# Two float32 half chunks per turn in place of one float32 chunk, in the narrow expert positions of an encoder trunk

## The chip, the cores and the metric

The kernel runs on one core of one Trainium2 chip. The metric is the device time of one execution in microseconds, the median of several runs; lower is better. Engines are named as the profile names them: PE is TensorE (matmuls), PEld its weight loads, DVE is VectorE, ACT is ScalarE, POOL is GpSimd, SP is SyncE, which here issues the weight loads from memory.

## The reference, cut to what matters

A two-layer encoder trunk on 256 tokens of width 1024. The part that the change touches is the last block, a mixture of eight SwiGLU experts of which each token takes two:

```python
def swiglu(xn, w_gu, w_down):
    g, u = jnp.split(xn @ w_gu, 2, axis=-1)
    return (jax.nn.silu(g) * u) @ w_down

def moe_swiglu(xn, router, w_gu, w_down):
    logits = (xn @ router).astype(jnp.float32)
    top_v, top_i = lax.top_k(logits, TOP_K)
    w = jax.nn.softmax(top_v, axis=-1)
    ...
    for e in range(N_EXPERTS):
        out = out + comb[..., e:e + 1] * swiglu(xn, w_gu[e], w_down[e])
    return out
```

`w_gu[e]` is 1024 x 7168 (gate and up side by side), `w_down[e]` is 3584 x 1024, all float32.

## The kernel before

**Precision.** A weight chunk is 128 x 2048 float32 (1 MB): four blocks of 128 x 512. `split` (line 152) cuts it into two halves of two blocks and, for each half, makes a rounded part `hi` on ACT (line 168, a cast to float32r) and a rest `lo = raw - hi` on DVE (line 169). Matmuls then run in float32r, one pass per block and part. `hi` and `lo` halves live in rings of four buffers each (lines 87, 88, `NPART = 4`), which is two chunks' worth; a buffer comes free when PE has read it. Raw chunks live in 11 buffers of one pool and 6 of another (line 55), 17 in all, loaded in order by SP (lines 143 and 939).

**Positions and turns.** The eight experts stand in eight positions, which `expert` (line 1127) takes one after the other. Positions 2, 4 and 6 are narrow (`NARROW`): their expert gets at most 64 tokens, and the activations' `hi` and `lo` stand side by side in one 128-column tile, so that one stationary tile carries both. The others are wide: 128 token slots, `hi` and `lo` in two tiles, so each block takes three passes (`moving`, line 207) where a narrow one takes two (`narrow`, line 1118: all `hi` blocks of a chunk, then all `lo` blocks).

A position has seven turns (loop at line 1208), one for each 512 columns of the hidden width. A turn takes six chunks in the order of their loads: two of the gate product (below: a, b), two of the up product (c, d), two of the down product of the turn before (e, f). In a narrow turn before the change, chunk d is not split: `gate_up` (line 1132) takes it with `whole_chunk` (line 1110) and runs four float32 matmuls on the raw data (line 1139; the trace shows two matmul records per block). The other five chunks are split: ten casts on ACT and ten subtractions on DVE per turn.

**What happens to a gate product in a narrow turn** (`gate`, line 1152): two copies on ACT bring the two 64-row halves of the result across (lines 1156, 1157), DVE adds them to the product (1158), ACT takes the silu (1159), and DVE multiplies with the up product (1163). `to_rows` (line 1166) turns that result by eight small matmuls (1172), which `side_by_side` (line 1049) casts on ACT (1053) and subtracts on DVE (1054); this is the stationary operand of the next `down` (line 1180).

**What sets the order.** The engines' instruction streams are not written out by hand. The framework's scheduler orders each engine's stream when the program is built, by program order as priority and by what its own timing model says is ready; each engine then runs its stream strictly in that order. `tc.issue_after(ins)` keeps what a block traces on the engine of `ins` behind `ins` in that stream, without a wait. `done[0]` is the last cast on ACT that `split` traced.

Of the kernel before, what the change touches and what calls it, by code (L numbers as in the profile page):

```python
# [25 lines left out]
F32 = mybir.dt.float32  # L26
F32R = mybir.dt.float32r
I32 = mybir.dt.int32
AF = mybir.ActivationFunctionType
# [3 lines left out]
P = 128  # L33
# [6 lines left out]
NE = 8  # L40
# [4 lines left out]
CH = 2048  # L45
# [4 lines left out]
HALF = CAP // 2  # L50
# [31 lines left out]
def _build(ctx, tc, io, cap):  # L82
# [7 lines left out]
    work = ctx.enter_context(tc.tile_pool(name="work", bufs=2))  # L90
    w2b, w1b = 4, 5
# [6 lines left out]
    V, S, G, PE = nc.vector, nc.scalar, nc.gpsimd, nc.tensor  # L98

    def f32(ap):  # L100
        return ap.bitcast(F32)
# [4 lines left out]
    def acc_tile(name="acc"):  # L106
        return psA.tile([P, 512], F32, tag="acc", name=name)
# [20 lines left out]
    def col(name, i=0):  # L128
        o = _OFF[name] + i
        return vec[:, o:o + 1]  # L130
# [18 lines left out]

    done = []  # L150

    def split(raw, n=CH, pieces=2, apart=()):

        cut = (n // 2 + P - 1) // P * P
        parts = []
        for a, b in ((0, cut), (cut, n)):
            if len(parts) in apart:  # L160
                both = rawp.tile([P, CH], F32R, tag="raw", name="apart")
                hi, lo = both[:, :CH // 2], both[:, CH // 2:]
            else:
                hi = hip.tile([P, CH // 2], F32R, tag="hi", name="hi")
                lo = lop.tile([P, CH // 2], F32R, tag="lo", name="lo")
            step = (b - a) * 2 // pieces
            for i in range(0, b - a, step):
                done[:] = (S.copy(hi[:, i:i + step], raw[:, a + i:a + i + step]),  # L168
                           V.tensor_sub(lo[:, i:i + step], raw[:, a + i:a + i + step],  # L169
                                        f32(hi[:, i:i + step])))  # L170
            parts.append((hi, lo))

        def at(a, b):
            hi, lo = parts[a >= cut]
            o = cut if a >= cut else 0
            return hi[:, a - o:b - o], lo[:, a - o:b - o]
        return at
# [44 lines left out]
    def halves(ps):  # L222
        return ps.rearrange("p (m t) -> p m t", m=2)
# [60 lines left out]
    def whole_of(t):  # L284
        return lambda k: t[:, k * T:(k + 1) * T]
# [269 lines left out]
    for g, w in enumerate(POOL_WINDOWS):  # L555
        left, right = w // 2, w - 1 - w // 2
        G.memset(invc[:, g, :], 1.0 / w)
        for t in list(range(left)) + list(range(T - right, T)):
            n = min(t + right, T - 1) + 1 - max(t - left, 0)
# [142 lines left out]
    ps = None  # L702
    for m in range(KD):
        if m % 2 == 0:
            ps = halves(acc_tile())
# [4 lines left out]
        for hf in range(2):  # L710
            w = split(load(io["ffn_down"][m, hf], half * P), half * P)
# [3 lines left out]
            for kk in range(half):  # L715
                k = hf * half + kk
                h, sl = hid[k // 8], slice((k % 8) * T, (k % 8 + 1) * T)
# [22 lines left out]
    for k in range(KD):  # L740
        last = V.scalar_tensor_tensor(a3[:, k * T:(k + 1) * T], hT[:, k, :], col("od_norm_mix", k), rb,
                               op0=ALU.mult, op1=ALU.mult)
    pw1 = [load(io["pw1"][c]) for c in range(2)]
    with tc.issue_after(last.ins):
        k1.append(split(load(io["wk"][1, 2])))
        ws = [Early(load(io["wv"][1, 2]), act_pair("wv")), early[2]]
# [44 lines left out]
    for c in range(KD):  # L791
        ps = product_whole(pw1[c] if c < 2 else load(io["pw1"][c]), whole_of(a3))
# [5 lines left out]
    last = conv31(KD - 1)  # L798
# [5 lines left out]
    ws = early[:2] + ws  # L804
# [18 lines left out]
    with tc.issue_after(last.ins):  # L823
        w = split(load(io["pw2"][0]))
# [21 lines left out]
    for k in range(KD):  # L846
# [5 lines left out]
        last = V.tensor_sub(p2[1][:, sl], x1, f32(p2[0][:, sl]))  # L852
# [5 lines left out]
    for c in range(1, 4):  # L858
        with tc.issue_after(last.ins):
            w = split(load(io["pw2"][c]))  # L860
# [75 lines left out]
    ahead = deque()  # L936
# [19 lines left out]
    for c in (1, 2):  # L956
        with tc.issue_after(turned[0].ins), tc.issue_after(turned[1].ins):
            w = split(wos[c])
# [148 lines left out]
    xg = big_tile("xg", F32R)  # L1107
    ht = big_tile("ht", F32R)

    def whole_chunk():  # L1110
        if not ahead:
            fetch()
        return ahead.popleft()

    def chunk(pieces=2):
        return split(whole_chunk(), pieces=pieces)

    def narrow(ps, xs, ws, first, last):

        n = len(xs)  # L1120
        for part in range(2):
            for i, (x, w) in enumerate(zip(xs, ws)):
                ins = PE.matmul(ps, x, w[part], start=first and i == part == 0,  # L1123
                                stop=last and part == 1 and i == n - 1)
        return ins

    def expert(e, g, following):
        nonlocal fn
        py = out_tiles()
        two = e in NARROW  # L1130

        def gate_up(j, gu):
            pz = acc_tile("gu")
            for kh in range(2):
                xs = [xg[:, k * P:(k + 1) * P] for k in range(kh * 4, kh * 4 + 4)]
                if two and gu == kh == 1:
                    w = whole_chunk()
                    for kk in range(4):
                        PE.matmul(pz, f32(xs[kk]), w[:, kk * 512:(kk + 1) * 512],  # L1139
                                  start=False, stop=kk == 3)  # L1140
                    continue
                w = chunk()
                ws = [w(kk * 512, (kk + 1) * 512) for kk in range(4)]
                if two:
                    narrow(pz, xs, ws, kh == 0, kh == 1)
                    continue
                moving(pz, [(xg[:, k * P:(k + 1) * P], xg[:, D + k * P:D + (k + 1) * P])
                            for k in range(kh * 4, kh * 4 + 4)],
                       ws, kh == 0, kh == 1)
            return pz  # L1150

        def gate(pg, pu):
            sg = work.tile([P, 512], F32, tag="w2", name="esg", bufs=w2b)
            if two:

                S.copy(sg[:HALF], pg[HALF:])
                S.copy(sg[HALF:], pg[:HALF])
                V.tensor_add(sg, sg, pg)
                S.activation(sg, sg, AF.Silu, scale=g.cw[:, 1:2])
            else:  # L1160
                S.activation(sg, pg, AF.Silu, scale=g.cw[:, 1:2])
            h = work.tile([P, 512], F32, tag="w2", name="eh", bufs=w2b)
            V.scalar_tensor_tensor(h, pu, g.cw[:, 1:2], sg, op0=ALU.mult, op1=ALU.mult)
            return h
# [12 lines left out]
            S.copy(ht[:, o:o + 512], pt)  # L1177
            V.tensor_sub(ht[:, o + 512:o + D], pt, f32(ht[:, o:o + 512]))

        def down(j, n):  # L1180
            w = chunk(4 if e == NE - 1 and j == 6 else 2)
            o = (j % 2) * D
            if two:
                return narrow(py[n], [ht[:, o + f * P:o + (f + 1) * P] for f in range(4)],
                              [w(f * 512, (f + 1) * 512) for f in range(4)], j == 0, j == 6)
            return moving(py[n],
                   [(ht[:, o + f * P:o + (f + 1) * P], ht[:, o + 512 + f * P:o + 512 + (f + 1) * P])
                    for f in range(4)],
                   [w(f * 512, (f + 1) * 512) for f in range(4)], j == 0, j == 6)
# [17 lines left out]
        h = None  # L1207
        for j in range(7):
            pg = gate_up(j, 0)
            if j:  # L1210
                to_rows(j - 1, h)
            pu = gate_up(j, 1)
            h = gate(pg, pu)
            if j:
                down(j - 1, 0)
                if j == 6:
                    to_rows(6, h)
                down(j - 1, 1)
            if following is not None and j in (3, 5):
                following.step(j)  # L1220
# [7 lines left out]
        last = down(6, 1)  # L1228
# [9 lines left out]
    g = Gather(0)  # L1238
# [88 lines left out]
    for e in range(NE):  # L1327
        following = Gather(e + 1) if e + 1 < NE else None
        expert(e, g, following)
        g = following  # L1330
# [174 lines left out]
```

## Time and profile before

| what | value |
|---|---|
| median of 3 runs | 1547.85 us (1547.59 to 1548.0) |
| the profiled execution, device time | 1547.42 us |
| its span in the trace | 1545.7 us |
| mean granted TensorE clock | 0.996 |
| DVE busy over the span | 1298.9 us (84%) |
| ACT busy over the span | 1052.1 us (68%) |
| POOL busy over the span | 148.1 us (10%) |

The profiled execution lasted 1.7 us longer than its span (launch and end lie outside) and 0.4 us less than the median. Busy shares are averages over stages with different limits: the expert block lies from about 591 us to 1532 us of the span, and its narrow and wide positions have to be read apart. A matmul's end in the trace is modelled, so the pace of PE is read from start to start.

### The profile page before, as it was taken

Reading aid. Unit: us, or ns where it says so; the run is one execution under the profiler, and the core shown is the slowest. Engines: PE = TensorE matmul, PEld = TensorE weight load, DVE = VectorE, ACT = ScalarE, POOL = GpSimd, SP = SyncE. Lnnn points to the kernel's source line nnn. Section 1 sums busy time; section 2 is a strip of 40 time slices with the busy share of each in tenths; the row PEclk is TensorE's granted clock in tenths of the full one; section 3 lists DMA queues with packets and bytes.
Section 4 is the critical chain, followed back from the end, with each engine's and each line's share of the span. In section 5 each row is a group of like instructions: output and inputs, shape, how many; then the busy total and the mean of one; then the engine's idle time right before and its main releaser. Section 6 shows DMA issues by size and latency. Waiting matters only on the chain.

```text
span 1545.7 us, 23643 instructions
## 1 busy us (share of the span) xinstructions
PE 1511.9 (98%) x8558; PEld 1294.3 (84%) x8558; DVE 1298.9 (84%) x1735; ACT 1052.1 (68%) x1381; POOL 148.1 (10%) x230
## 2 busy tenths in 40 slices
PE   8999999999999999999999999999999999999996
PEld 8899999999998998888888768888667888667885
DVE  7876677776898868999999989889889888889897
ACT  6555554455585647777777877777777777777775
POOL 4710100001394210000000000000000000000000
PEclk9999999999999999999999999999999999999998
DMA  9654454336536566998999999998999999999950
GB/s 370 269 191 164 142 186 166 120 113 236 188 134 244 174 264 221 371 377 334 373 366 342 397 422 412 381 375 331 403 402 376 367 361 343 408 392 382 364 191 30
DMA packets 65213, 451.42 MB, mean 292 GB/s; under 512 B 7360, under 2 KB 7488, under 8 KB 12480
## 3 DMA queue, kind: packets, MB, share of 16 engines
q1 hardware_dynamic: 65088, 449.83, 76.6%
q8 instruction: 69, 1.13, 0.3%
q14 instruction: 56, 0.46, 0.1%
HBM read 448.75 MB, written 1.05 MB: 291 GB/s over the span
## 4 chain that ended last, share of the span: by engine, by line
PE 82%; DVE 9%; POOL 3%; issue 3%; ACT 2%; DMA 1%; SPq 0%; DVEq 0%; POOLq 0%; ACTq 0%
PE gu L211 8%; PE gu L212 8%; PE gu L216 8%; PE acc L205 7%; PE acc L203 7%; PE acc L204 7%; DVE lo L169 6%; PE gu L1139 5%; PE gu L1123 4%; PE py L211 4%; PE py L216 4%; PE py L212 4%; PE py L1123 3%; POOL part L779 2%; PE gx L1042 1%
## 5 line engine op out<-in xcount | busy, mean ns | idle before, releaser
L169 DVE TENSOR_TENSOR lo<-raw,hi 128x1024 fp32r<-128x1024 f32 (+3 forms) x573 | 671.6, 1208 | 113.9 <-ACT hi L168 103.6
L168 ACT CAST hi<-raw 128x1024 fp32r<-128x1024 f32 (+3 forms) x573 | 565.4, 1030 | 212.9 <-PE acc L204 89.4
L169 DVE TENSOR_TENSOR lo<-spare,hi 128x1024 fp32r<-128x1024 f32 (+1 forms) x226 | 260.9, 1198 | 24.4 <-ACT hi L168 20.4
L168 ACT CAST hi<-spare 128x1024 fp32r<-128x1024 f32 (+1 forms) x226 | 221.5, 1035 | 23.6 <-PE gu L212 11.7
L211 PE MATMUL gu<-hi,xg 128*128 128x512 f32 x560 | 218.8, 391 | 0.0
L212 PE MATMUL gu<-hi,xg 128*128 128x512 f32 x560 | 218.3, 390 | 0.0
L216 PE MATMUL gu<-lo,xg 128*128 128x512 f32 x560 | 154.2, 391 | 0.6 <-DVE lo L169 0.6
L216 PEld LDWEIGHTS gu<-lo,xg 128*128 128x128 f32 x560 | 104.7, 188 | 23.9 <-DVE lo L169 1.9
L211 PEld LDWEIGHTS gu<-hi,xg 128*128 128x128 f32 x560 | 105.1, 188 | 22.2 <-ACT hi L168 0.2
L212 PEld LDWEIGHTS gu<-hi,xg 128*128 128x128 f32 x560 | 105.1, 188 | 21.8
L211 PE MATMUL py<-hi,ht 128*128 128x512 f32 x280 | 111.1, 398 | 0.0
L212 PE MATMUL py<-hi,ht 128*128 128x512 f32 x280 | 109.3, 390 | 0.0
L205 PE MATMUL acc<-a2h,lo 128*128 128x256 f32 x336 | 95.2, 283 | 0.0
L204 PE MATMUL acc<-a2l,hi 128*128 128x256 f32 x336 | 95.2, 283 | 0.0
L203 PE MATMUL acc<-a2h,hi 128*128 128x256 f32 x336 | 95.1, 283 | 0.0
L1401 POOL TENSOR_TENSOR fo<-accum,fn 128x512 f32<-128x512 f32 x2 | 2.5, 1272 | 948.9 <-DVE accum L1205 948.9
L1123 PE MATMUL gu<-lo,xg 128*128 128x512 f32 x252 | 80.4, 411 | 7.9 <-DVE lo L169 7.6
L216 PE MATMUL py<-lo,ht 128*128 128x512 f32 x280 | 84.0, 395 | 0.0
L1123 PE MATMUL gu<-hi,xg 128*128 128x512 f32 x252 | 71.3, 397 | 0.0
L1123 PEld LDWEIGHTS gu<-lo,xg 128*128 128x128 f32 x252 | 43.4, 188 | 31.5 <-DVE lo L169 25.2
L203 PEld LDWEIGHTS acc<-a2h,hi 128*128 128x128 f32 x336 | 64.5, 192 | 0.0
L205 PEld LDWEIGHTS acc<-a2h,lo 128*128 128x128 f32 x336 | 64.5, 192 | 0.0
(424 smaller groups left out, 3171.9 us busy)
## 6 DMA issues: line engine op xcount, KB each, us to landing
raw<-in_moe_gu SPq DMA_DIRECT2D x139, 1024.0 KB, 7.1
spare<-in_moe_gu SPq DMA_DIRECT2D x85, 1024.0 KB, 7.2
raw<-in_moe_down SPq DMA_DIRECT2D x78, 1024.0 KB, 7.4
spare<-in_moe_down SPq DMA_DIRECT2D x32, 1024.0 KB, 7.0
raw<-in_ffn_gu SPq DMA_DIRECT2D x22, 1024.0 KB, 4.8
raw<-in_pw SPq DMA_DIRECT2D x12, 1024.0 KB, 4.8
raw<-in_ffn_down SPq DMA_DIRECT2D x16, 704.0 KB, 4.1
raw<-in_wk SPq DMA_DIRECT2D x8, 1024.0 KB, 7.3
```

The lines of the kernel that those rows point to most:

```text
L168: done[:] = (S.copy(hi[:, i:i + step], raw[:, a + i:a + i + step]), V.tensor_sub(lo[:, i:i + step], raw[:, a + i:a + i + step], f32(hi[:, ...
L169: V.tensor_sub(lo[:, i:i + step], raw[:, a + i:a + i + step], f32(hi[:, i:i + step])))
L203: PE.matmul(ps, a[0], b[0], start=first, stop=False)
L204: PE.matmul(ps, a[0], b[1], start=False, stop=False)
L205: PE.matmul(ps, a[1], b[0], start=False, stop=last)
L211: PE.matmul(ps, a[0], b[0], start=first and i == 0, stop=False)
L212: PE.matmul(ps, a[1], b[0], start=False, stop=False)
L216: ins = PE.matmul(ps, a[0], b[1], start=False, stop=last and i == n - 1)
L779: G.tensor_add(part, part, prod)
L1042: PE.matmul(px[:, kk * P:(kk + 1) * P], xt[:, t * D + d0:t * D + d0 + P], oh[:, t, :], start=t == 0, stop=t == 1)
L1123: ins = PE.matmul(ps, x, w[part], start=first and i == part == 0, stop=last and part == 1 and i == n - 1)
L1139: PE.matmul(pz, f32(xs[kk]), w[:, kk * 512:(kk + 1) * 512], start=False, stop=kk == 3)
```

## The change

In a narrow turn, all six chunks now go through `split`, which learns to leave one of its halves whole (`whole=(1,)`: no cast, no subtraction; the raw half is handed out). The second half of chunk c (the first chunk of the up product) and the second half of chunk f (the second chunk of the down product) are left whole, and chunk d is split. `narrow` takes the blocks with a `hi` and a `lo` first and then the raw blocks, as float32. The two copies and the addition of the gate product move out of `gate` into `fold`, which is traced right after chunk c is split, with the copies queued on ACT behind the cast of c's first half. Silu is queued on ACT behind the casts of chunk e, which is therefore split ahead of `gate`. Wide positions keep their code.

```diff
--- before.py
+++ after.py
@@ -149,7 +149,8 @@
 
     done = []
 
-    def split(raw, n=CH, pieces=2, apart=()):
+    def split(raw, n=CH, pieces=2, apart=(), whole=()):
+
 
 
 
@@ -157,6 +158,9 @@
         cut = (n // 2 + P - 1) // P * P
         parts = []
         for a, b in ((0, cut), (cut, n)):
+            if len(parts) in whole:
+                parts.append(None)
+                continue
             if len(parts) in apart:
                 both = rawp.tile([P, CH], F32R, tag="raw", name="apart")
                 hi, lo = both[:, :CH // 2], both[:, CH // 2:]
@@ -171,6 +175,8 @@
             parts.append((hi, lo))
 
         def at(a, b):
+            if parts[a >= cut] is None:
+                return raw[:, a:b]
             hi, lo = parts[a >= cut]
             o = cut if a >= cut else 0
             return hi[:, a - o:b - o], lo[:, a - o:b - o]
@@ -1107,21 +1113,17 @@
     xg = big_tile("xg", F32R)
     ht = big_tile("ht", F32R)
 
-    def whole_chunk():
+    def chunk(pieces=2, whole=()):
         if not ahead:
             fetch()
-        return ahead.popleft()
-
-    def chunk(pieces=2):
-        return split(whole_chunk(), pieces=pieces)
+        return split(ahead.popleft(), pieces=pieces, whole=whole)
 
     def narrow(ps, xs, ws, first, last):
 
-        n = len(xs)
-        for part in range(2):
-            for i, (x, w) in enumerate(zip(xs, ws)):
-                ins = PE.matmul(ps, x, w[part], start=first and i == part == 0,
-                                stop=last and part == 1 and i == n - 1)
+        todo = [(x, w[part]) for part in range(2) for x, w in zip(xs, ws) if isinstance(w, tuple)]
+        todo += [(f32(x), w) for x, w in zip(xs, ws) if not isinstance(w, tuple)]
+        for i, (x, w) in enumerate(todo):
+            ins = PE.matmul(ps, x, w, start=first and i == 0, stop=last and i == len(todo) - 1)
         return ins
 
     def expert(e, g, following):
@@ -1129,36 +1131,35 @@
         py = out_tiles()
         two = e in NARROW
 
-        def gate_up(j, gu):
+        def gate_up(j, gu, pg=None):
             pz = acc_tile("gu")
             for kh in range(2):
                 xs = [xg[:, k * P:(k + 1) * P] for k in range(kh * 4, kh * 4 + 4)]
-                if two and gu == kh == 1:
-                    w = whole_chunk()
-                    for kk in range(4):
-                        PE.matmul(pz, f32(xs[kk]), w[:, kk * 512:(kk + 1) * 512],
-                                  start=False, stop=kk == 3)
-                    continue
-                w = chunk()
+                w = chunk(whole=(1,) if two and gu and kh == 0 else ())
                 ws = [w(kk * 512, (kk + 1) * 512) for kk in range(4)]
+                if two and gu and kh == 0:
+
+                    with tc.issue_after(done[0].ins):
+                        pg = fold(pg)
                 if two:
                     narrow(pz, xs, ws, kh == 0, kh == 1)
                     continue
                 moving(pz, [(xg[:, k * P:(k + 1) * P], xg[:, D + k * P:D + (k + 1) * P])
                             for k in range(kh * 4, kh * 4 + 4)],
                        ws, kh == 0, kh == 1)
-            return pz
+            return (pg, pz) if gu else pz
+
+        def fold(pg):
+
+            sg = work.tile([P, 512], F32, tag="w2", name="esg", bufs=w2b)
+            S.copy(sg[:HALF], pg[HALF:])
+            S.copy(sg[HALF:], pg[:HALF])
+            V.tensor_add(sg, sg, pg)
+            return sg
 
         def gate(pg, pu):
-            sg = work.tile([P, 512], F32, tag="w2", name="esg", bufs=w2b)
-            if two:
-
-                S.copy(sg[:HALF], pg[HALF:])
-                S.copy(sg[HALF:], pg[:HALF])
-                V.tensor_add(sg, sg, pg)
-                S.activation(sg, sg, AF.Silu, scale=g.cw[:, 1:2])
-            else:
-                S.activation(sg, pg, AF.Silu, scale=g.cw[:, 1:2])
+            sg = pg if two else work.tile([P, 512], F32, tag="w2", name="esg", bufs=w2b)
+            S.activation(sg, pg, AF.Silu, scale=g.cw[:, 1:2])
             h = work.tile([P, 512], F32, tag="w2", name="eh", bufs=w2b)
             V.scalar_tensor_tensor(h, pu, g.cw[:, 1:2], sg, op0=ALU.mult, op1=ALU.mult)
             return h
@@ -1177,8 +1178,9 @@
             S.copy(ht[:, o:o + 512], pt)
             V.tensor_sub(ht[:, o + 512:o + D], pt, f32(ht[:, o:o + 512]))
 
-        def down(j, n):
-            w = chunk(4 if e == NE - 1 and j == 6 else 2)
+        def down(j, n, w=None):
+            if w is None:
+                w = chunk(4 if e == NE - 1 and j == 6 else 2, (1,) if two and n else ())
             o = (j % 2) * D
             if two:
                 return narrow(py[n], [ht[:, o + f * P:o + (f + 1) * P] for f in range(4)],
@@ -1209,10 +1211,12 @@
             pg = gate_up(j, 0)
             if j:
                 to_rows(j - 1, h)
-            pu = gate_up(j, 1)
-            h = gate(pg, pu)
+            pg, pu = gate_up(j, 1, pg)
+            w = chunk() if j and two else None
+            with tc.issue_after(done[0].ins) if two else nullcontext():
+                h = gate(pg, pu)
             if j:
-                down(j - 1, 0)
+                down(j - 1, 0, w)
                 if j == 6:
                     to_rows(6, h)
                 down(j - 1, 1)
```

## Rows read from the trace of the kernel before

**Rows 1.** The page, part 1: busy time of PE and PEld (share) over the whole span.

```profile
PE 1511.9 (98%) x8558; PEld 1294.3 (84%) x8558; DVE 1298.9 (84%) x1735; ACT 1052.1 (68%) x1381; POOL 148.1 (10%) x230
```

**Rows 2.** Windows, positions 2, 3, 4, 6: us, PE, PEld, DVE, ACT, POOL busy, clock, DMA, GB/s.

```profile
838.00:940.00 102.00, 101.15 (x437) 74.38 (x437) 94.16 (x100) 82.89 (x101) 0.00 (x0) 1.00 1.00 400
940.00:1067.00 127.00, 126.81 (x591) 105.12 (x590) 115.73 (x115) 97.01 (x109) 0.00 (x0) 1.00 0.98 378
1067.00:1175.00 108.00, 103.89 (x429) 71.16 (x428) 92.24 (x98) 79.82 (x98) 0.00 (x0) 1.00 0.97 388
...
1302.00:1410.00 108.00, 103.93 (x429) 71.17 (x428) 92.48 (x96) 79.95 (x99) 0.00 (x0) 1.00 0.98 391
```

**Rows 3.** Windows view, single turns: one of position 4, two of position 2.

```profile
1109.34:1124.90 15.56, 14.71 (x58) 9.53 (x56) 13.11 (x14) 11.73 (x14) 0.00 (x0) 1.00 0.99 395
...
873.40:886.40 13.00, 13.00 (x56) 9.55 (x55) 12.88 (x13) 11.70 (x14) 0.00 (x0) 1.00 0.96 377
886.40:899.40 13.00, 13.00 (x56) 9.54 (x55) 12.72 (x13) 11.23 (x14) 0.00 (x0) 1.00 1.01 425
```

**Rows 4.** Timeline of ACT, position 4: start, us, instruction, count, [idle before, releaser].

```profile
1110.89 0.59 ACT L1156 COPY esg<-gu 64x512 f32<-64x512 f32 x1 [1.58 <-PE gu L1123]
...
1112.96 0.72 ACT L1159 ACTIVATE esg<-esg,cw 128x512 f32<-128x512 f32 x1 [0.90 <-DVE esg L1158]
1113.59 1.97 ACT L168 CAST hi<-spare 128x1024 fp32r<-128x1024 f32 x2
...
1118.83 0.37 ACT L1053 CAST ht<-ht 128x256 fp32r<-128x256 f32 x1 [1.36 <-PE ht L1172]
1119.09 5.79 ACT L168 CAST hi<-raw 128x1024 fp32r<-128x1024 f32 x6
1126.44 0.58 ACT L1156 COPY esg<-gu 64x512 f32<-64x512 f32 x1 [1.55 <-PE gu L1123]
1127.04 0.58 ACT L1157 COPY esg<-gu 64x512 f32<-64x512 f32 x1
```

**Rows 5.** Timeline of DVE, the same turn.

```profile
1112.25 0.68 DVE L1158 TENSOR_TENSOR esg<-esg,gu 128x512 f32<-128x512 f32 x1
1114.65 1.23 DVE L169 TENSOR_TENSOR lo<-spare,hi 128x1024 fp32r<-128x1024 f32 x1 [1.72 <-ACT hi L168]
1116.60 0.75 DVE L1163 SCALAR_TENSOR_TENSOR eh<-gu,cw,esg 128x512 f32<-128x512 f32 x1 [0.72 <-PE gu L1139]
...
1120.67 0.42 DVE L1054 TENSOR_TENSOR ht<-ht 128x256 fp32r<-128x256 f32 x1
1121.01 6.89 DVE L169 TENSOR_TENSOR lo<-raw,hi 128x1024 fp32r<-128x1024 f32 x6
1127.81 0.68 DVE L1158 TENSOR_TENSOR esg<-esg,gu 128x512 f32<-128x512 f32 x1
```

**Rows 6.** Timeline of PE, the same turn.

```profile
1112.96 3.60 PE L1139 MATMUL gu<-raw,xg 128*128 128x512 f32 x8
1116.00 1.49 PE L1123 MATMUL py<-hi,ht 128*128 128x512 f32 x4
1117.33 0.62 PE L1123 MATMUL py<-lo,ht 128*128 128x512 f32 x2
1117.79 1.00 PE L1172 MATMUL ht<-kept,eh 128*128 128x64 f32 x8
```

**Rows 7.** Waits in positions 2 and 4: us in total, times, longest.

```profile
DVE lo L169 <- ACT hi L168: 3.8, 4, 1.7
...
DVE lo L169 <- ACT hi L168: 10.3, 6, 1.7
```

**Rows 8.** Timeline of ACT, a 13.00 us turn of position 2.

```profile
883.08 2.94 ACT L168 CAST hi<-raw 128x1024 fp32r<-128x1024 f32 x3
885.92 0.72 ACT L1159 ACTIVATE esg<-esg,cw 128x512 f32<-128x512 f32 x1
```

**Rows 9.** Waits of SP's load queue, positions 2 to 6: us in total, times, longest.

```profile
SPq L147 <- PE gu L1139: 76.7, 21, 5.0
```

## The prediction, made before the changed kernel was run

> **What bounds the kernel now.** The page's first part gives PE as busy for 98% of the span [rows 1], which would leave no room. The windows by position, read next, say otherwise for the narrow positions: position 3, a wide one, has PE at 126.81 of 127.00 us, but positions 4 and 6 at 103.9 of 108.0, with the weight loads at 71 of 108 where the wide one has 105 of 127 [rows 2]. The granted clock is 1.00 everywhere, the upper level (2.4 GHz), so no clock hangs on this change. One level deeper, single turns: a turn of position 4 lasts 15.56 us with DVE busy for 13.11; two turns of position 2, with the same instructions but for one to three, last 13.00 us each, PE and DVE both full [rows 3]. So a narrow turn has 2.56 us of waits which it can do without.
>
> One rule of the Trainium skill stands against the first reading: it (Perfetto Trace Analysis, Identifying the Most-Contended Engine) calls matmul busy time a poor measure of how near PE is to its limit and judges by the weight loads' share. By matmul busy time a turn could give 0.85 us (15.56 less 14.71), by the share of the weight loads (61% in the long turn, 73% in the short ones) the whole 2.56. The short turns side with the page [rows 3].
>
> Where the 2.44 us of DVE's idle time lie is in the timelines of one long turn [rows 4 to 6]. The copies of the gate product start at 1110.89; DVE adds at 1112.25; silu stands on ACT directly behind the copies, so ACT waits 0.90 for the addition and only then casts the first half of e, for which DVE has waited 1.72. DVE then takes the product with up (L1163) and waits 0.72 for it, since PE is in the float32 chunk. The long wait comes six times in position 4, the row of position 6 reads the same, and in position 2 once: its other three waits sum to 2.1 [rows 7]. That makes 13 turns. In the short turns three casts stand ahead of silu [rows 8].
>
> **The change, part by part.** *Work.* Ten casts and ten subtractions a turn before (five chunks), ten after (six chunks less two halves): 0. PE has 40 float32r passes and 8 float32 records before and after. A record costs 0.43: the eight and the four passes behind them take 4.37 us from 1112.96 to 1117.33, the passes at 0.23 each (two from 1117.33 to 1117.79) 0.92 of it, which leaves 3.45 for eight [rows 6]. So a half chunk is 1.72 us of PE without any cast, at two places instead of 3.45 at one. The sum of work is 0.
>
> *Silu behind e's casts.* It removes DVE's wait of 1.72. ACT casts d and e (four at 0.97, from six in 5.79) and then takes silu (0.72), while DVE still has the subtractions of d and e to do, so DVE reaches the product with up late enough for both of its inputs: the wait of 0.72 goes as well. Behind silu on ACT stands f's one cast, covered by the same subtractions.
>
> *Copies behind c's first cast.* They already stand behind all of c's and the rest (six casts, then the copies [rows 4]). What is new is that only c's first half is left between b and the copies: d's casts come later in program order. ACT waits at the copies for PE to end the gate product, with d's casts queued behind. That is a new wait for DVE: it has one subtraction (c) to cover what before were two.
>
> *The turned product.* L1053, the cast of what PE turns (L1172), stands ahead of the next turn's six casts and ACT waits 1.36 for it [rows 4]. Before, that cost nothing: ACT was four casts ahead and DVE had three subtractions left. After the change silu, and with it L1163, come later, by a whole chunk's casts, and L1053 with them. I see nothing in the edit that moves it behind the next casts. So the new chain of a turn, from the start of the copies, is: two copies at 0.60, 1.20; the first cast of d and the subtraction that follows 1.06 later (1113.59 to 1114.65), 2.26; four subtractions at 1.13 (six from 1121.01 to 1127.81), 6.79; L1163, 0.75, 7.54; L1172 and L1053 1.04 after its start (1117.79 to 1118.83), 8.58; 0.26 until the next cast, 8.84; 1.06 to the first subtraction of a, 9.90; four more, 14.43; and 0.90 from the end of b's last subtraction (1121.01 plus 4.53) to the next copies (1126.44), **15.33 us**, against 15.56 [rows 4 to 6]. Gain 0.23 a turn.
>
> *Bounds.* If f's two `hi` passes stand ahead of L1172 on PE, up to 0.46 is added to 8.58 and the gain is gone (15.79). If L1053 doesn't hold up the casts, the turn is 14.44 (below). I take 15.33, between the two and nearer to the order that the rows show. Turns of position 2 that are short now: 0, within 1 us together either way.
>
> *Loads.* The raw halves of c and f are held until PE has read them, two chunks a turn where it was one; SP waited 21 times for such a buffer [rows 9]. No engine's wait in the narrow positions is put down to a load, and 17 buffers are nearly three turns' worth. At 15.3 us a turn of six 1.05 MB chunks needs 411 GB/s, and 425 were moved in a short turn [rows 3]: 0.
>
> Sum: 13 turns at 0.23 are 3.0 us, off the profiled execution's 1547.4, which gives 1544.4. The median of the runs is 0.4 above that execution: **1544.9 us**.
>
> **The rivals.** *A, the turned product is out of the way* (L1053 behind a's casts). Then only the wait at the copies is left: after 7.54 DVE goes on with f (8.67), a and b (13.20), L1054 (0.34, from 1120.67 to 1121.01) and the 0.90: 14.44 us, 1.12 less, 14.6 us over 13 turns, 1533.2 with the 0.4 added [rows 5]. For it: the scheduler decides by its own model, and the margin between L1053 and a's cast is small. Against it: the order in rows 4.
>
> *C, all waits go.* If a cast of d slips ahead of the copies as well, a turn is as short as DVE's work, 13.11 [rows 3]: 2.45 less, 31.9 us, 1516. It is what the Trainium skill's rule above (Perfetto Trace Analysis) holds possible. Against it: two things have to fall right at once.
>
> *D, slower: L1172 lands behind f's float32 half on PE.* Then L1053 starts not at 8.58 but after f's subtraction (8.67), two passes (0.46), the half chunk (1.72) and 1.04, at 11.9, with all casts of the next turn behind it: 3.3 us more, a turn of 18.6, 3.1 over now, 1588 over 13 turns and 1554 if it strikes two of them. It decides from the point where L1053 starts later than 8.81. For it: the margin is 0.23 us. Against it: L1163 is ready before f's subtraction is done, so L1172 has a gap to go into.
>
> That the change does nothing of what it says can't be for silu, which is tied to a cast; for the copies it can, as they stand behind c's casts already.
>
> **How the numbers follow.** The forecast (B, 1544.9, its own range 1540 to 1549 by the bounds above) has 0.50, A 0.30, C 0.08, D 0.12. A measurement can tell 0.2% from no change, 3.1 us, so B lies on that edge: of its 0.50, 0.20 is faster, 0.26 the same, 0.04 slower. Faster: 0.30 + 0.08 + 0.20 = 0.58; same 0.26; slower 0.12 + 0.04 = 0.16. The range takes in A with some room (1528) and B with its gain lost and a little more (1551); C and D, 0.20, stay outside.
>
> **What the profile after would show.** Right: on ACT c's cast, copies, four casts, silu, one cast, L1053 with a wait, then a; DVE's wait of 1.7 gone from behind L1158, and in its place one of about 1 us ahead of it and one of about 1 ahead of a's first subtraction; narrow turns of about 15.3 us. A shows L1053 behind a cast of a and turns of 14.4; C shows DVE without waits; D shows L1172 behind L1123's float32 records. Wrong altogether: other turns than the narrow ones changed, or casts that wait for loads.

## The result and the profile after

The changed kernel takes 1558.57 us (median of 4 runs, 1556.7 to 1561.54) where the kernel before takes 1547.92: slower, the ratio is 1.0071 [1.0053, 1.0088]. The forecast was 1544.9, with 1551 as its upper end. The profiled execution took 1556.7 us with a span of 1555.0, 9.3 us more than before.

Where the 9.3 us lie is read from the starts of the gate products' first instruction on ACT, turn by turn (the first copy in a narrow turn, silu in a wide one), in both traces:

| stretch | before, us | after, us | difference |
|---|---|---|---|
| all ahead of the first narrow copies | 843.75 | 842.71 | -1.04 |
| position 2, its six intervals | 79.21 | 81.92 | +2.71 |
| position 2's last copies to the third silu of position 3 | 53.51 | 53.02 | -0.49 |
| position 4, first interval | 10.31 | 10.94 | +0.63 |
| position 4, the other five | 77.66 | 79.54 | +1.88 |
| its last copies to the third silu of position 5 | 53.51 | 54.92 | +1.41 |
| position 6, first interval | 10.75 | 11.55 | +0.80 |
| position 6, the other five | 77.65 | 79.63 | +1.98 |
| its last copies to the third silu of position 7 | 53.54 | 54.92 | +1.38 |

These sum to 9.26; nothing else moved. The first row is no sure gain: in the profiles of the variants below, that point lies anywhere between 843.38 and 845.26 us. So there are three losses: the steady turns (3.9), the ends and beginnings of positions (3.7 net of the gain behind position 2), and one turn of position 2 (3.1, of which its other turns give 0.4 back).

**The steady turn.** The windows view of the changed kernel, one turn of position 4 (columns as in [rows 2]):

```profile
1109.00:1124.84 15.84, 15.07 (x58) 9.47 (x57) 13.32 (x14) 11.73 (x15) 0.00 (x0) 1.00 0.99 390
```

15.84 us against 15.56, with the same work [rows 3]. Its ACT stream, from the timeline of a turn of position 6 (in the changed kernel the copies are L1155 and L1156, the cast L172, silu L1162, the turned product's cast L1059):

```profile
1321.00 0.58 ACT L1155 COPY esg<-gu 64x512 f32<-64x512 f32 x1 [1.53 <-PE gu L1126]
...
1322.19 3.89 ACT L172 CAST hi<-raw 128x1024 fp32r<-128x1024 f32 x4
1325.99 0.72 ACT L1162 ACTIVATE esg<-esg,cw 128x512 f32<-128x512 f32 x1
1326.61 1.04 ACT L172 CAST hi<-raw 128x1024 fp32r<-128x1024 f32 x1
1330.03 0.37 ACT L1059 CAST ht<-ht 128x256 fp32r<-128x256 f32 x1 [2.38 <-PE ht L1173]
1330.30 1.99 ACT L172 CAST hi<-raw 128x1024 fp32r<-128x1024 f32 x2
...
1336.83 0.58 ACT L1155 COPY esg<-gu 64x512 f32<-64x512 f32 x1 [1.69 <-PE gu L1126]
```

This is the forecast's order to the instruction: copies, four casts, silu, one cast, the turned product's cast with a wait (2.38 us; 1.36 before [rows 4]), the next turn's five. The DVE timeline of the same turn:

```profile
1322.20 0.69 DVE L1157 TENSOR_TENSOR esg<-esg,gu 128x512 f32<-128x512 f32 x1 [0.85 <-ACT esg L1156]
1323.27 4.63 DVE L173 TENSOR_TENSOR lo<-raw,hi 128x1024 fp32r<-128x1024 f32 x4 [0.38 <-ACT hi L172]
1327.82 0.74 DVE L1164 SCALAR_TENSOR_TENSOR eh<-gu,cw,esg 128x512 f32<-128x512 f32 x1
...
1330.43 0.42 DVE L1060 TENSOR_TENSOR ht<-ht 128x256 fp32r<-128x256 f32 x1 [0.74 <-ACT ht L1059]
1331.38 2.36 DVE L173 TENSOR_TENSOR lo<-raw,hi 128x1024 fp32r<-128x1024 f32 x2 [0.52 <-ACT hi L172]
```

The waits of 1.72 and 0.72 [rows 5] are gone. In their place stand 0.85 and 0.38 at the copies, 0.74 and 0.52 at the turned product: 2.49 us where there were 2.44. The wait was cut in four, not removed.

**The turn in position 2.** The second interval of position 2 went from 14.88 to 18.01 us. PE's timeline and then DVE's show why:

```profile
857.21 0.70 PE L1126 MATMUL gu<-hi,xg 128*128 128x512 f32 x2
860.57 1.20 PE L1126 MATMUL py<-hi,ht 128*128 128x512 f32 x4 [2.66 <-DVE ht L1060]
```

```profile
856.69 1.22 DVE L173 TENSOR_TENSOR lo<-raw,hi 128x1024 fp32r<-128x1024 f32 x1
857.83 2.36 DVE L173 TENSOR_TENSOR lo<-spare,hi 128x1024 fp32r<-128x1024 f32 x2
860.10 0.42 DVE L1060 TENSOR_TENSOR ht<-ht 128x256 fp32r<-128x256 f32 x1
```

PE stands for 2.66 us before the first down product, because the scheduler put the turned product's subtraction (0.42) behind two subtractions of later chunks (2.36) on DVE.

### The profile page after: what moved, and what is told of

Its sections match the earlier page's. It is cut to its first block, busy times and chain, and to the rows that moved or that the text cites. A ratio compares the mean times of both kernels' runs of the same rounds, so it can differ in the third digit from the quotient of the medians.

```text
span 1555.0 us, 23659 instructions
## 1 busy us (share of the span) xinstructions
PE 1518.4 (98%) x8558; PEld 1291.9 (83%) x8558; DVE 1303.5 (84%) x1735; ACT 1052.6 (68%) x1381; POOL 148.2 (10%) x230
## 5 line engine op out<-in xcount | busy, mean ns | idle before, releaser
L172 ACT CAST hi<-raw 128x1024 fp32r<-128x1024 f32 (+3 forms) x570 | 564.5, 1030 | 216.3 <-PE acc L210 88.1
L173 DVE TENSOR_TENSOR lo<-spare,hi 128x1024 fp32r<-128x1024 f32 (+1 forms) x229 | 265.3, 1202 | 23.3 <-ACT hi L172 15.6
L172 ACT CAST hi<-spare 128x1024 fp32r<-128x1024 f32 (+1 forms) x229 | 225.5, 1034 | 36.9 <-PE gu L218 21.9
L217 PE MATMUL gu<-hi,xg 128*128 128x512 f32 x560 | 220.3, 393 | 0.0
L218 PE MATMUL gu<-hi,xg 128*128 128x512 f32 x560 | 218.7, 390 | 0.0
L222 PE MATMUL gu<-lo,xg 128*128 128x512 f32 x560 | 154.9, 391 | 0.0
L217 PEld LDWEIGHTS gu<-hi,xg 128*128 128x128 f32 x560 | 105.2, 188 | 22.6 <-issue 0.7
L218 PEld LDWEIGHTS gu<-hi,xg 128*128 128x128 f32 x560 | 105.2, 188 | 22.4 <-issue 0.7
L222 PEld LDWEIGHTS gu<-lo,xg 128*128 128x128 f32 x560 | 105.0, 188 | 22.2
L1126 PE MATMUL gu<-lo,xg 128*128 128x512 f32 x294 | 94.8, 412 | 8.0 <-DVE lo L173 7.8
L1126 PE MATMUL gu<-hi,xg 128*128 128x512 f32 x294 | 98.7, 440 | 0.4 <-ACT hi L172 0.4
L1126 PEld LDWEIGHTS gu<-lo,xg 128*128 128x128 f32 x294 | 50.9, 188 | 36.0 <-DVE lo L173 28.3
L1126 PEld LDWEIGHTS gu<-hi,xg 128*128 128x128 f32 x294 | 53.5, 188 | 29.8 <-ACT hi L172 12.8
```

Source lines behind the costliest of these rows:

```text
L217: PE.matmul(ps, a[0], b[0], start=first and i == 0, stop=False)
L218: PE.matmul(ps, a[1], b[0], start=False, stop=False)
L222: ins = PE.matmul(ps, a[0], b[1], start=False, stop=last and i == n - 1)
L1126: ins = PE.matmul(ps, x, w, start=first and i == 0, stop=last and i == len(todo) - 1)
```

## The experiments

Four theories were open after the result. **1**: the turned product's cast, late because silu is late, holds the next turn's casts on ACT and so sets the turn. **2**: the wait at the copies sets it. **3**: PE itself has more to do. **4**: in position 2 it is the order on DVE, 5 (later) the place of the float32 work. Line numbers of L1059 and its like shift by a few in the variants.

### e1: the turned product's cast behind the next turn's a

```diff
@@ the changed kernel
+                if not gu and kh == 0:
+                    first[:] = done
...
             if j:
-                to_rows(j - 1, h)
+                with tc.issue_after(first[0].ins) if two else nullcontext():
+                    to_rows(j - 1, h)
```

> The changed kernel, with one more order edge: in narrow turns the cast of the turned product (L1059 of the changed kernel) is queued on ACT behind the casts of the next turn's first chunk (a). In the stream of positions 4 and 6 it then stands behind two of those casts; position 2 keeps its order. Theory 1 (the turned product's cast, late because silu is late, holds up the next turn's casts on ACT and through them DVE, and that is the 15.84 us turn): a steady turn falls to about 14.4 us, all of it 1540 (1536 to 1545). Theory 2 (the wait at the copies, which have only half of c ahead of them, sets the turn): the turn stays above 15.5, 1555 or more. Theory 3 (PE itself is longer with the two float32 halves): no change, 1558.

Measured: 1553.41 us, ratio 1.0032 [1.002, 1.0045]. From its ACT timeline in position 4:

```profile
1116.57 0.58 ACT L1159 COPY esg<-gu 64x512 f32<-64x512 f32 x1 [2.16 <-PE gu L1126]
...
1122.19 2.94 ACT L172 CAST hi<-raw 128x1024 fp32r<-128x1024 f32 x3
1125.62 0.37 ACT L1059 CAST ht<-ht 128x256 fp32r<-128x256 f32 x1 [0.49 <-PE ht L1177]
...
1131.52 0.58 ACT L1159 COPY esg<-gu 64x512 f32<-64x512 f32 x1 [2.16 <-PE gu L1126]
```

The cast starts as late as before (9.05 us after the copies), two casts now pass it, and the turn falls by 0.89 to 14.95. So the cast did hold up a, as theory 1 says, but both of its numbers were missed: the turn stays 0.5 above what it gave, and the time 13 us (position 2 lost more in this run, see e2). The copies, with 2.16 us of waiting, look like a second limit; e4 and e6 try that.

### e2: the half chunks alone

```diff
@@ the changed kernel
-                if two and gu and kh == 0:
-                    with tc.issue_after(done[0].ins):
-                        pg = fold(pg)
...
-            sg = pg if two else work.tile(...)
-            S.activation(sg, pg, AF.Silu, ...)
+            sg = fold(pg) if two else work.tile(...)
+            S.activation(sg, sg if two else pg, AF.Silu, ...)
...
-            w = chunk() if j and two else None
-            with tc.issue_after(done[0].ins) if two else nullcontext():
-                h = gate(pg, pu)
+            h = gate(pg, pu)
             if j:
-                down(j - 1, 0, w)
+                down(j - 1, 0)
```

> Only the work part of the change: half chunks c and f as float32, d split; copies, addition and silu are traced in the gate as before, with no order edges. In positions 4 and 6 the ACT stream has five casts, the copies, two casts (d), silu, three casts, the turned product; position 2 has the changed kernel's order, cast for cast. Theory 1: silu is two casts earlier than in the changed kernel, the product with up about one subtraction earlier, the turned product's cast at about 7.5 instead of 9.0 us after the copies, and a steady turn is 14.4 us: 1543 (1538 to 1548). Theory 2 (copies): they stand at the same place as in the changed kernel, so the turn stays at 15.8 and the time at 1558. Theory 3 (PE longer): 1558 too.

Measured: 1551.85 us, ratio 1.0024 [1.0014, 1.0033]. The steady turn is 15.15 us: shorter than before the change (15.56), longer than theory 1 gave (14.4) and shorter than theories 2 and 3 did (15.8). So in steady turns the half chunks gain 0.4 and the order edges lose 0.7. Yet the kernel is slower than before the change: its position 2 lost 5.0 us from the first narrow copies to the third wide silu (137.76 against 132.72), for a reason of its own. PE's timeline there:

```profile
861.88 2.08 PE L1126 MATMUL py<-hi,ht 128*128 128x512 f32 x4 [2.67 <-DVE ht L1060]
863.75 1.91 PE L1126 MATMUL py<-lo,ht 128*128 128x512 f32 x4
```

The windows view over 9 us of it, of e2 and then of the changed kernel:

```profile
861.00:870.00 9.00, 8.12 (x22) 5.75 (x23) 5.08 (x6) 4.08 (x4) 0.00 (x0) 0.62 0.73 294
```

```profile
860.00:869.00 9.00, 8.43 (x37) 6.43 (x38) 6.88 (x8) 6.20 (x7) 0.00 (x0) 1.00 0.96 348
```

PE waited 2.67 us for L1060, as in the changed kernel, but here the granted clock then fell: 0.62 over the 9 us, a mixture of the two levels, and four passes took 2.08 us (1.20 in the changed kernel's profile). The interval is 20.83 us instead of 18.01. In the profile of e1 it is 20.81, in that of e4 19.6. The four runs of the changed kernel list mean clocks of 0.996 and 0.993; the lower value belongs to the two longest, 1558.97 and 1561.54. Only one of the four, at 0.996, was profiled, so that the clock fell at this place in the two long ones is likely, not shown.

### e3: silu alone behind e's casts

```diff
@@ the kernel before
                 V.tensor_add(sg, sg, pg)
-                S.activation(sg, sg, AF.Silu, scale=g.cw[:, 1:2])
+                with tc.issue_after(done[0].ins):
+                    S.activation(sg, sg, AF.Silu, scale=g.cw[:, 1:2])
...
+            w = chunk() if j and two else None
             h = gate(pg, pu)
             if j:
-                down(j - 1, 0)
+                down(j - 1, 0, w)
```

> The kernel before with one order edge: silu is queued behind the casts of chunk e; the whole chunk d stays float32 and the copies keep their place behind all of c's casts. ACT: six casts, copies, two casts (e), silu, two casts (f), turned product. Theory 1: the wait of 1.7 us behind the addition goes, the turned product's cast comes at about 7.5 us after the copies, as early as before, and a steady turn is 14.3 us instead of 15.56: 1533 (1529 to 1540). Theory 2 (copies) says the same here, as two subtractions of c cover them. A theory that silu's place does not matter, because DVE's wait only moves: 1546 to 1550.

Measured: 1547.48 us, ratio 0.9996 [0.9987, 1.0005]: the same as before, a miss for theory 1 as I had put numbers to it. Its ACT timeline:

```profile
1111.46 0.59 ACT L1156 COPY esg<-gu 64x512 f32<-64x512 f32 x1 [0.74 <-PE gu L1123]
...
1120.30 0.37 ACT L1053 CAST ht<-ht 128x256 fp32r<-128x256 f32 x1 [3.13 <-PE ht L1173]
...
1127.11 0.58 ACT L1156 COPY esg<-gu 64x512 f32<-64x512 f32 x1 [0.75 <-PE gu L1123]
```

The turned product's cast is not at 7.5 but at 8.84 us after the copies, behind a wait of 3.13, and the turn is 15.65. The wait that silu had caused went to the turned product. PE's timeline shows how:

```profile
1117.89 1.08 PE L1123 MATMUL py<-lo,ht 128*128 128x512 f32 x4
1118.81 0.62 PE L1123 MATMUL py<-hi,ht 128*128 128x512 f32 x2
1119.27 1.00 PE L1173 MATMUL ht<-kept,eh 128*128 128x64 f32 x8
```

DVE's product starts as early as before the change (5.77 us after the copies, 5.71 before), but the scheduler put all of e's passes and f's two `hi` passes ahead of the turned product, ten where there were six [rows 6], so that its matmuls start 7.81 us after the copies instead of 6.90. That the turned product's cast then sets the turn, as theory 1 says, shows in a difference: from that cast to the next copies it is 6.81 us here, 6.80 in the changed kernel (1330.03 to 1336.83).

### e4: copies behind d's casts

```diff
@@ the changed kernel
-                if two and gu and kh == 0:
+                if two and gu and kh == 1:
                     with tc.issue_after(done[0].ins):
                         pg = fold(pg)
```

> The changed kernel with the copies traced one chunk later, queued behind both casts of d instead of behind the cast of c: ACT has seven casts, copies, two casts (e), silu, one cast (f), turned product. Theory 1: the turned product's cast comes at about 7.6 us after the copies (four fewer things between), a short wait of DVE ahead of a stays, the turn is 14.4 us and the time 1540. Theory 2 (copies): the wait at the copies is covered by d's subtractions, the turn is 14.4 or less, 1540 or less. Theory 3 (PE): 1558.

Measured: 1544.19 us, ratio 0.9975 [0.9966, 0.9984]. Steady turns are 14.62 us, 1.2 less than in the changed kernel. This one edge turns the change from a loss into a gain, though position 2 still has its long turn (19.6). The edge also takes back what the ends had lost: from the last copies to the third wide silu it is 53.46 us in position 4 (54.92 in the changed kernel, 53.51 before the change), with PE busy throughout. Theory 3 is out; theories 1 and 2, which gave the same here, were 0.2 us a turn and 4 us in all too low. The copies cost no wait any more, the turned product still does:

```profile
1114.33 0.58 ACT L1154 COPY esg<-gu 64x512 f32<-64x512 f32 x1
...
1121.92 0.37 ACT L1059 CAST ht<-ht 128x256 fp32r<-128x256 f32 x1 [2.83 <-PE ht L1172]
```

### e5: f's subtraction behind the turned product's

```diff
@@ the changed kernel (rows[-1] is the subtraction L1060 of the last to_rows)
-                w = chunk(4 if e == NE - 1 and j == 6 else 2, (1,) if two and n else ())
+                with tc.issue_after(rows[-1].ins) if two and n else nullcontext():
+                    w = chunk(4 if e == NE - 1 and j == 6 else 2, (1,) if two and n else ())
```

> The changed kernel with one order edge on DVE: f's subtraction (second chunk of the down product) is queued behind the subtraction of the turned product. In the second turn of position 2 that puts L1060 ahead of two subtractions instead of behind them; positions 4 and 6 keep their order. Theory 4 (what position 2 lost is PE waiting about 2.7 us for L1060 behind those two subtractions, after which the granted clock falls in some executions): the second turn of position 2 falls from 18.0 to 20.8 us to about 15.5, the clock stays at 1.00 there, the time is 1554 (1552 to 1556) and the runs lie closer together than 1556.7 to 1561.5. Rival (PE lacks cover there because a half chunk is short, wherever L1060 stands): the turn stays at 18 or more, 1558.

Measured: 1558.73 us (1557.68 to 1559.75), ratio 1.0067 [1.0053, 1.0081]. The edge worked at the place meant, the time did not move. L1060 now stands ahead of the two subtractions, as DVE's timeline shows:

```profile
857.71 1.23 DVE L173 TENSOR_TENSOR lo<-raw,hi 128x1024 fp32r<-128x1024 f32 x1
858.84 0.43 DVE L1060 TENSOR_TENSOR ht<-ht 128x256 fp32r<-128x256 f32 x1
```

The windows view of that stretch has the granted clock at 1.00:

```profile
855.00:873.00 18.00, 17.60 (x77) 12.76 (x76) 17.85 (x19) 14.36 (x18) 0.00 (x0) 1.00 1.00 397
```

The second interval falls to 16.67 us: of the 3.13 that it had lost in the changed kernel's profile, 1.34 hung on L1060's place, while the other 1.79 against the kernel before were not tried. But the scheduler also laid out the position's later turns anew: its last turn now has the order of positions 4 and 6, and the stretch to the third silu of position 3 is 54.94 us instead of 53.02. That gives the gain back.

### e6, e7: the edges together

e6 has the edges of e1 and e4, e7 those of e1, e4 and e5.

> Both order edges of the first two order runs together: copies behind d's casts and the turned product's cast behind the next turn's a. Theory 1 and 2 together (each of the two waits on ACT is a limit of its own, and the second takes over when the first goes): a steady turn of positions 4 and 6 falls from 14.6 (copies behind d alone) to about 13.6, near PE's own work of 13.5, and the time from 1544 to 1535 (1532 to 1538). Rival (with the copies behind d the turned product no longer limits anything): 14.6 and 1544.

> The three edges together: copies behind d, turned product's cast behind a, f's subtraction behind the turned product's. If the three causes are separate places, the gains add: 1535 less about 4.5 is 1530 (1527 to 1534), turns of 13.6 in positions 4 and 6, no turn of 18 in position 2.

Measured: e6 1536.95 us, ratio 0.9927 [0.9913, 0.994]; e7 1532.72 us, ratio 0.99 [0.9884, 0.9915]. A steady turn is 13.50 us in both. The windows view of e7, such a turn of position 4 and the stretch of position 2:

```profile
1095.18:1108.68 13.50, 13.50 (x57) 9.92 (x56) 13.50 (x14) 11.83 (x14) 0.00 (x0) 1.00 1.01 421
855.00:873.00 18.00, 17.60 (x76) 12.46 (x75) 17.90 (x19) 14.34 (x18) 0.00 (x0) 1.00 0.99 401
```

PE is full. The waits at the copies and at the turned product are two limits: to take away one alone gave 0.89 us a turn (e1) and 1.22 (e4), to take away both 2.34. Here the third edge does pay, 4.2 us between e6 and e7: position 2's second interval is 16.67 instead of 20.67 (in e6's profile the granted clock fell there as well, 0.81 over 855 to 873 us), and with the two other edges its last turn and the stretch behind it cost only 0.3 us.

### e8: the kernel before, silu and the turned product moved

This is e3 with the edge of e1, without any half chunk.

> The kernel before (whole float32 chunk d) with silu behind e's casts and the turned product's cast behind the next turn's a. Theory 1 (silu alone gained nothing because the turned product's cast moved from 7.9 to 8.9 us after the copies and held up a): with it behind a the steady turn falls from 15.65 to about 14.4 and the time from 1547.5 to 1532 (1529 to 1537). Rival (the whole float32 chunk ahead of the product with up is the limit): 15.6 and 1547.

Measured: 1537.4 us, ratio 0.9929 [0.9916, 0.9943], steady turns of 14.48 us; the turn is as theory 1 has it, the time 0.4 us above its range. So e3's gain had indeed been held up by the turned product's cast. The kernels with half chunks reach 13.50 (e6, e7), about 1 us a turn less, but they have the copies behind d's casts too, so what the halves alone are worth is not shown; e6, with its long turn in position 2, is no faster in all (1536.95).

### e9: the turned product ahead of f on PE

```diff
@@ the changed kernel (turned[0] is the last small matmul, L1173)
-            if j:
+            if j == 1 or j and not two:
                 to_rows(j - 1, h)
...
-                if j == 6:
-                    to_rows(6, h)
+                if j == 6 or two:
+                    to_rows(j, h)
...
             if two:
+              with tc.issue_after(turned[0].ins) if n else nullcontext():
                 return narrow(py[n], ...)
```

> The changed kernel with one edge on PE: the eight small matmuls of the turned product (L1173) stand ahead of f's products instead of behind f's two hi passes; ACT keeps its order in positions 4 and 6. Theory 1 with the term that the forecast left out (the 0.46 us of f's hi passes in front of L1173 add to every turn): the turned product's cast comes at 8.6 us after the copies instead of 9.0, the turn falls from 15.83 to 15.4, as forecast, and the time to 1553 (1550 to 1556). Rival (the turn is set by the copies or by PE's work and L1059 only follows): 15.8 and 1558.

Measured: 1558.24 us, ratio 1.007 [1.0056, 1.0084]. The steady turn is 15.57, 0.27 less than in the changed kernel and not 0.46 less. First PE in the changed kernel, then PE in e9:

```profile
1328.53 0.63 PE L1126 MATMUL py<-hi,ht 128*128 128x512 f32 x2
1328.99 1.00 PE L1173 MATMUL ht<-kept,eh 128*128 128x64 f32 x8
```

```profile
1122.53 0.73 PE L1126 MATMUL py<-lo,ht 128*128 128x512 f32 x2 [0.17 <-DVE lo L173]
1123.19 1.10 PE L1175 MATMUL ht<-kept,eh 128*128 128x64 f32 x8
```

With f out of the way PE still waits for DVE's product (L1175 starts 7.62 us after the copies, L1173 did at 7.99). The cast starts at 8.76 after the copies (1124.33) and the next copies come 6.81 later, the same 6.8 for the third time. The whole time did not move: between the two profiles, the ten steady turns of positions 4 and 6 gained 3.1 us, position 2 came out 1.7 us longer, and the first narrow copies came 1.3 us later, which no edge accounts for.

### e10 to e12: where the float32 work lies, and the slots' step

e10 is e7 with `(1,) if two and n and j < 6`, so that the last down chunk of a narrow position is split whole. e11 is e7 with `following.step(5)` traced in turn 6, behind b's casts. e12 has both.

> The kernel with all three edges, and the last down chunk of each narrow position (second chunk of hidden block 6) split whole instead of half float32. Theory 5 (the change moved float32 work of PE out of the first turn of a position into its end, where PE is full, and that is the longer handover to the wide position): 1.72 us of PE become 0.91 there, the stretch from the last narrow copies to the third wide gate product falls from 53.5 by 0.8 in each of three positions, 1532.7 becomes 1530.3 (1529 to 1531.5). Rival (DVE comes late into the wide position): one more cast and subtraction make it longer, 1533 to 1536.

> The kernel with all three edges, and the small transposes and copies of the next position's slots (the step at turn 5) traced in turn 6 behind b's casts in narrow positions. The long turn of 15.13 us in positions 4 and 6 comes from the cast of the slots' matrix (L1098), which stands on ACT ahead of the next turn's casts: it falls to 13.5, the last interval grows by less than that, 1532.7 becomes 1530 (1528 to 1532). Rival (PE's own work for the step is the 1.6 us): no change.

> The two runs before it together on the kernel with all three edges: 1527.5 (1525 to 1530) if both hold and add.

Measured: e10 1529.49 us, ratio 0.9883 [0.9868, 0.9898]; e11 1530.69, 0.9889 [0.9873, 0.9904]; e12 1529.36, 0.9879 [0.9864, 0.9894]. In e10 the stretch from a position's last copies to the third wide silu falls from 53.49 to 52.64 us behind each of positions 2, 4 and 6: 0.85 each, the price that theory 5 gave the half chunk. The changed kernel's longer stretch (54.92) it is not, as e7 has 53.49 with the same half chunk still in it. In e11 the long interval falls from 15.13 to 14.30, not to 13.5, and what holds the other 0.8 was not tried. The row of e7 that it goes back to is this one on ACT:

```profile
1130.00 0.37 ACT L1098 CAST oT<-ot 128x256 fp32r<-128x256 f32 x1 [3.06 <-PE ot L1096]
```

By whole times the two do not add: e12 is as fast as e10 within the intervals. By stretch they do: position 4, from its first copies to the third wide silu, takes 133.77 us in e7, 132.86 in e10, 133.02 in e11 and 132.13 in e12. What e12 gains so is lost ahead of all that the edits touch, where its profile comes to the first narrow copies at 845.26 us and e10's at 843.38. These versions are 1.1 to 1.2% faster than the kernel before.

## Why the prediction was wrong

**Right: the order and the mechanism.** ACT's stream after the change is the one forecast for case B, and so are the two new waits and their places: one at the copies, with only half of c as cover, one ahead of a, behind the turned product. The two old waits went. Work did not change. Loads did not matter: SP waits for PE's reading of raw halves in two rows now (22 and 11 times, below, where it was 21 [rows 9]), and in the waits of the narrow positions no engine waits for a load.

```profile
SPq L147 <- PE gu L1126: 54.3, 22, 4.4
SPq L147 <- PE py L1126: 21.6, 11, 2.5
```

**Wrong: the step "15.33 us".** I took the value without f's two `hi` passes in front of L1172 and kept 0.46 only as a bound; the turn is 15.84. In the turn of position 6 shown above, DVE's product starts 6.82 us after the copies (6.79 in the forecast), PE's turned matmuls 1.17 behind it (0.75), their cast 1.04 behind that (1.04), and the next copies 6.80 later (6.75): of the 0.50 that the sum is short, 0.42 lie where f's two `hi` passes stand (1328.53 to 1328.99). So the case that I had put aside as a bound is the one that came. e9, which takes these passes away, wins back 0.27 of it, as the matmuls start 0.37 earlier but their cast comes 1.14 behind them instead of 1.04; what its turn is still above 15.33, 0.24, are hand-overs that I counted from single rows (0.03 up to the product, 0.05 from there to PE, 0.10 to the cast, 0.06 to the next copies). With a margin of 0.23 between gain and loss, a chain of nine steps could not carry a sign. What the runs put in place of that sum is a difference: where the turned product's cast stands ahead of a, DVE waits for it and the copies then wait for PE, the next copies follow 6.80 to 6.81 us later (the changed kernel, e3, e9); in e4, where seven casts stand ahead of the copies and these wait for nothing, it is 7.03.

**Wrong: "turns of position 2: 0, within 1 us".** It was +2.7 in the profile, and +5.5 in e2's, where the clock fell as well. I had read position 2's good turns as a proof that waits can go, and not asked what order the scheduler would give them after the change. e2 has the long turn without any order edge, so it came with the half chunks; e5 and e7 show that L1060's place on DVE is a part of it (18.01 to 16.67 us, and no fall of the clock). Why the interval is not 14.88 again stays open.

**Wrong: "the sum of work is 0".** It is, over a position, but the float32 passes moved from the whole chunk d, of which the first turn has one, to halves of f, of which the end has one more. The first intervals got one more half to subtract (+0.63 and +0.80); that their loss is that extra half was not tried by itself. The end got 1.72 us of float32 in place of 0.91 of float32r passes. Where PE is full, as in e7, that costs its length: e10 takes it away and gets 0.85 back each time. But the +1.4 to the third silu in the changed kernel is not this work: e4, e6 and e7 have the same passes there and 53.46 to 53.50 us in positions 4 and 6, so it is the waits of the last turn, which go with the copies' edge.

**The rivals.** A did not come, but e1, which makes it so, gives 14.95 and not 14.44: I had let DVE's chain alone set that turn, but in e1 it is PE, late after the wait at the copies, that sets it: its timeline shows no wait from 1124.11 to the next copies at 1131.52, for which DVE then stands 1.45. C (13.11) came nearly true at 13.50 once both waits were taken away; the Trainium skill's reading (Perfetto Trace Analysis, Identifying the Most-Contended Engine), that the share of the weight loads shows the room, is borne out: 60% in the turn of 15.84, 73% in the full one of 13.50 (9.92 of 13.50). D's order did not come: L1173 stands ahead of f's `lo` and float32 passes. But its border of 8.81, from which the forecast counted a loss, was crossed without it, by 9.03.

## What to carry to other kernels

Where each engine runs its stream strictly in order and hands small results round, a wait that is taken away by moving one instruction can come back at the next small instruction in that stream, as in e3; so move them as a set (here copies, silu and the turned product's cast), and look at what stands directly behind each wait, and ahead of the work that it waits for. Against the kernel before, the changed kernel with one edge more stood at +0.7% to -0.3% (e5, e1, e4), with that set at -0.7% (e6), and with f's subtraction moved as well at -1.0% (e7). And count work by stretch, not by sum: equal work, moved to where PE is already full, costs its whole length (0.85 us in e10 for an estimated 0.81).

## What the runs showed that I had not expected

A wait of PE of 2.7 us in the middle of dense work was followed in some executions by a fall of the granted clock and in others not: 1.00 over the 9 us after it in the changed kernel's profile, 0.62 in e2's, after waits of 2.66 and 2.67 us. Four more profiles have that wait, 2.67 or 2.68 us: the clock stayed at 1.00 in e9's and fell in those of e1, e4 and e6 (0.62, 0.81 and 0.81 in windows there). Where it fell, the same turn took 19.6 to 20.8 us instead of 18.0. What decides whether it falls is not shown. e7, whose position 2 has no such wait, has 1.00 there, and its runs lie within 2.2 us of each other (1531.84 to 1534.0) where the changed kernel's lie within 4.8.
